# The up products of an MLP by Strassen's algorithm: seven block products in place of eight

## The chip, the cores and the metric

The kernel runs on one core of a Trainium2 chip. A core has a matrix engine (TensorE, PE in the rows), a vector engine (VectorE, DVE), a scalar engine (ScalarE, ACT), a general engine (GpSimd, POOL) and a queue engine (SyncE, SP) that here only starts transfers. Each works off its own instructions strictly in the order in which they stand and waits for the others by semaphores; that order is fixed when the program is built. The metric is the time on the device of one whole execution, in microseconds (us), as the median of several runs.

## The reference, cut to what matters

One decoder block: a gated linear-attention branch and a sparse-attention branch on 512 tokens and 16 extra leading tokens, merged, projected, and then an MLP. The change touches the MLP, and what leads to it:

```python
mix = jnp.einsum('btd,de->bte', merged, w_out[l])
h = h + _rmsnorm(mix, post_mix_norm[l])
n2 = _rmsnorm(h, pre_mlp_norm[l])
u = jnp.square(jax.nn.relu(jnp.einsum('btd,df->btf', n2, w_up[l])))   # 1024 -> 4096
h = h + _rmsnorm(jnp.einsum('btf,fd->btd', u, w_down[l]), post_mlp_norm[l])   # 4096 -> 1024
```

All data are float32. TensorE takes operands of a reduced float32 type, so the kernel splits every operand into a high part (the rounded value) and a low part (what is left) and makes each product of three: high times high, high times low, low times high.

## The kernel before, in words

Everything ahead of the output projection (the attention branches and the merge) is untouched.

**Weights.** `wload` (L90) is how every weight block of 128 x 1024 numbers comes in: SP starts its transfer into one of two `raw` buffers, ScalarE writes the high part (`S.copy`, L99), VectorE writes the low part, `raw` minus high (L100). The pairs lie in five rotating buffers `hl`, or, with `spare`, in two other places.

**Output projection.** `proj_rows` (L517) computes it in two halves of 512 columns. The second half, the tiles `ob`, goes token tile by token tile (four tiles t of 128 tokens); behind each, `mix_done` (L1042) computes the token's norm by a chain of tiny instructions on VectorE and adds the residual into `h2`, and `mix_more` (L1051) transposes the tile on TensorE (`n2t`) and writes it, times the norm weight, as high and low parts `n2h` and `n2l`, in pieces of 128 x 128. The row norm of `n2` itself is applied at the very end (`mlp_scale`, L1065, four more chains of tiny instructions).

**Up.** 4096 hidden columns in four groups g of 1024, each group eight tiles of 128 (`up_tile`, L1094). A tile is 8 x 3 = 24 matmuls with 512 tokens as moving columns: weights of `w_up` stand, `n2` moves. Then ScalarE takes the ReLU out of PSUM (L1106), VectorE squares it (L1108), and `split` makes high and low parts (ScalarE L705, VectorE L706). The first four tiles of group 0 are done in two halves of 256 tokens, so that TensorE can start on the first two token tiles.

**Down.** `down` (L1124) multiplies a group's hidden tiles with `w_down`, 512 output columns at a time, over four accumulators in PSUM (`d`), 24 matmuls of 512 columns each per accumulator, and adds each accumulator into `acc` on VectorE (L1133; group 0 is copied by ScalarE, L1131). The program computes up(0), up(1), down(0), up(2), down(1), up(3), down(2), down(3), so that up is always a group ahead. The last group's second half, the tiles `d3b`, goes token tile by token tile, each with its norm and its output.

**What sets the order.** The calls are recorded in program order; a scheduler then orders the instructions of each engine by that priority, as operands and buffers come free in its own model. Tiles of one tag share that tag's buffers, and a new tile of the tag waits for the last reader of the old one. The tags that matter here: `s1` to `s6` (one large buffer each), `tb` and `st` (two buffers of 128 x 1024 each), `raw` (two), `hl` (five).

Of the kernel before, what the change touches and what calls it, by code (L numbers as in the profile page):

```python
# [38 lines left out]
def hybrid_block(ctx: ExitStack, tc: tile.TileContext, io: dict):  # L39
# [50 lines left out]
    def wload(src, n, name, spare=False):  # L90
# [929 lines left out]
    n2h = mp.tile([P, KT, L], F32R, name="n2h")  # L1020
    n2l = mp.tile([P, KT, L], F32R, name="n2l")
# [28 lines left out]

    def mix_more(t):  # L1051
        nonlocal last_n2

        ts = slice(t * P, (t + 1) * P)
        for b in range(2):
# [4 lines left out]
            for k in range(4):  # L1060
                kk = 4 * b + k
                last_n2 = S.activation(n2h[:, kk, ts], ps[:, k * P : (k + 1) * P], AF.Copy, scale=gmT[:, kk : kk + 1])
                V.scalar_tensor_tensor(n2l[:, kk, ts], ps[:, k * P : (k + 1) * P], gmT[:, kk : kk + 1], f(n2h[:, kk, ts]), ALU.mult, ALU.subtract)

    def mlp_scale(t):  # L1065
        s1 = wk.tile([P, 1], F32, tag="s1", name=f"s1{t}", bufs=2)
        S.activation(gx[:, 2 + t % 2, :], h2[:, t, :], AF.Square, accum_out=s1)
# [26 lines left out]
    def up_tile(g, i, w, c0, n):  # L1094
        uh, ul = us[g]
        nm = f"up{g}{i}{c0}"
        hi, lo = w
        pt = ptile(nm)[:, :n]
        ms = slice(c0, c0 + n)
        for k in range(KT):  # L1100
            ws = slice(k * P, (k + 1) * P)
            TE.matmul(pt, hi[:, ws], n2h[:, k, ms], start=(k == 0), stop=False)  # L1102
            TE.matmul(pt, hi[:, ws], n2l[:, k, ms], start=False, stop=False)  # L1103
            TE.matmul(pt, lo[:, ws], n2h[:, k, ms], start=False, stop=(k == KT - 1))  # L1104
        r = wk.tile([P, T], F32, tag="cv", name=f"r{nm}", bufs=2)[:, :n]
        S.activation(r, pt, AF.Relu)  # L1106
        u = wk.tile([P, T], F32, tag="y", name=f"u{nm}", bufs=2)[:, :n]
        V.tensor_tensor(u, r, r, ALU.mult)  # L1108
        split(uh[:, i, ms], ul[:, i, ms], u)

    def up(g):
        uh = slots.tile([P, 8, L], F32R, tag=("s2", "s6")[g % 2], name=f"uh{g}")
        ul = slots.tile([P, 8, L], F32R, tag=("s1", "s5")[g % 2], name=f"ul{g}")
        us[g] = (uh, ul)
        first = 4 if g == 0 else 0
        ws = [wload(io["w_up"][8 * g + i], 1024, f"up{g}{i}", spare=i % 2 == 1) for i in range(first)]
        for c0 in (0, 256):
            for i in range(first):
                up_tile(g, i, ws[i], c0, 256)
        for i in range(first, 8):  # L1120
            up_tile(g, i, wload(io["w_up"][8 * g + i], 1024, f"up{g}{i}"), 0, L)

    def down(g):
        uh, ul = us[g]  # L1124
        last = g == NG - 1

        def d_evac(pt, t, c0, n, i):
            cs = slice(c0, c0 + n)
            a = acc[t][:, cs]
            if g == 0:  # L1130
# [102 lines left out]
```

## Time and profile before

| what | value |
|---|---|
| median of 3 runs | 1063.04 us (1062.64 to 1063.52) |
| the profiled execution | 1063.86 us, of which span 1062.2 us |
| PE busy | 1040.1 us (98%) |
| DVE busy | 682.0 us (64%) |
| ACT busy | 460.9 us (43%) |
| stretch of the MLP (683 us to the end) | 379 us |

The span runs from the first to the last instruction in the profile; what lies around it is 1063.86 - 1062.2 = 1.7 us. Busy shares are means over the span. Matmuls overlap in the profile (a matmul's duration is longer than the distance to the next one's start), so TensorE's pace is read from the distance of starts, and the same holds for VectorE, where one instruction's end lies over the next one's start.

### The profile page before, as it was taken

To read this page: it belongs to the slowest core of one execution; us is meant where nothing else is said; L and a number is where in the kernel's file an instruction comes from. 1 tells how busy PE (TensorE), PEld (TensorE's weight loads), DVE (VectorE), ACT (ScalarE), POOL (GpSimd) and SP (SyncE) were. 2 spreads that over 40 slices of the span, in tenths; PEclk is the share of its full clock that TensorE was granted. 3 is DMA by queue.
4 is the path that set the end of the run, shared out by engine and by line. 5 is a ranking of instruction groups with operands and counts; after the bars stand their busy time and mean duration, and the time that the engine had idled before them with its cause. 6 is when DMAs were issued, how large, how long until landed. Compare 5 with 4: busy or idle time off the path is not lost.

```text
span 1062.2 us, 15893 instructions
## 1 busy us (share of the span) xinstructions
PE 1040.1 (98%) x6249; PEld 900.7 (85%) x6249; DVE 682.0 (64%) x1502; ACT 460.9 (43%) x854; POOL 61.7 (6%) x85
## 2 busy tenths in 40 slices
PE   6999999999999999999999999999999999999996
PEld 6999999999997888898888888898888888888885
DVE  6797899516789999857967464794431343343346
ACT  5555565443268722346755332473432431242131
POOL 4202302100000000000000000000000000000022
PEclk9999999998999999999999999999999999999999
DMA  5433424210123133322111325133233323332332
GB/s 180 134 102 95 124 86 134 63 41 2 41 83 117 46 94 99 100 80 80 60 60 41 99 93 204 60 103 95 84 96 99 96 85 98 99 90 88 99 99 80
DMA packets 28235, 96.44 MB, mean 91 GB/s; under 512 B 3632, under 2 KB 3968, under 8 KB 28160
## 3 DMA queue, kind: packets, MB, share of 16 engines
q1 hardware_dynamic: 25440, 87.51, 26.5%
q0 software_dynamic: 2720, 7.92, 2.9%
q8 instruction: 49, 0.80, 0.3%
q14 instruction: 26, 0.21, 0.1%
HBM read 90.14 MB, written 5.28 MB: 90 GB/s over the span
## 4 chain that ended last, share of the span: by engine, by line
PE 89%; DVE 5%; ACT 2%; DMA 2%; issue 1%; SPq 0%; DVEq 0%; ACTq 0%
PE up L1103 5%; PE up L1104 5%; PE up L1102 5%; PE d L505 4%; PE d L504 4%; PE d L506 4%; PE pa_dense L891 2%; PE pa_dense L890 2%; PE pa_dense L889 2%; PE pa_q L196 1%; PE pa_q L194 1%; PE pa_q L195 1%; PE pa_bg L194 1%; PE pa_bg L196 1%; PE pa_bg L195 1%; PE bd L1012 1%
## 5 line engine op out<-in xcount | busy, mean ns | idle before, releaser
L1103 PE MATMUL up<-n2l,hi_up 128*128 128x512 f32 (+1 forms) x288 | 106.9, 372 | 0.0
L1102 PE MATMUL up<-n2h,hi_up 128*128 128x512 f32 (+1 forms) x288 | 106.6, 371 | 0.0
L1104 PE MATMUL up<-n2h,lo_up 128*128 128x512 f32 (+1 forms) x288 | 106.6, 371 | 0.0
L100 DVE TENSOR_TENSOR lo_up<-raw_up,hi_up 128x1024 fp32r<-128x1024 f32 x32 | 39.2, 1226 | 71.1 <-PE up L1103 52.9
L100 DVE TENSOR_TENSOR lo_d<-raw_d,hi_d 128x1024 fp32r<-128x1024 f32 x24 | 29.4, 1227 | 78.4 <-PE d L505 56.0
L504 PE MATMUL d<-hi_d,uh 128*128 128x512 f32 x192 | 75.9, 396 | 0.0
L506 PE MATMUL d<-hi_d,ul 128*128 128x512 f32 x192 | 75.9, 395 | 0.0
L505 PE MATMUL d<-lo_d,uh 128*128 128x512 f32 x192 | 75.9, 395 | 0.0
L1106 ACT ACTIVATE rup<-up 128x512 f32<-128x512 f32 (+1 forms) x36 | 19.9, 552 | 99.5 <-PE up L1104 99.4
L1103 PEld LDWEIGHTS up<-n2l,hi_up 128*128 128x128 f32 x288 | 54.2, 188 | 10.3
L1102 PEld LDWEIGHTS up<-n2h,hi_up 128*128 128x128 f32 x288 | 54.2, 188 | 10.3
L1104 PEld LDWEIGHTS up<-n2h,lo_up 128*128 128x128 f32 x288 | 54.1, 188 | 10.3
L99 ACT CAST hi_d<-raw_d 128x1024 fp32r<-128x1024 f32 x24 | 25.2, 1050 | 59.6 <-PE d L506 59.6
L99 ACT CAST hi_up<-raw_up 128x1024 fp32r<-128x1024 f32 x32 | 33.4, 1045 | 24.6 <-PE d L506 22.7
L504 PEld LDWEIGHTS d<-hi_d,uh 128*128 128x128 f32 x192 | 36.1, 188 | 8.8
L506 PEld LDWEIGHTS d<-hi_d,ul 128*128 128x128 f32 x192 | 36.1, 188 | 8.7
L505 PEld LDWEIGHTS d<-lo_d,uh 128*128 128x128 f32 x192 | 36.1, 188 | 8.7
L889 PE MATMUL pa_dense<-nhi,hi_dense 128*128 128x512 f32 x96 | 39.3, 409 | 0.0
L890 PE MATMUL pa_dense<-nlo,hi_dense 128*128 128x512 f32 x96 | 38.0, 396 | 0.0
L548 PE MATMUL pb_z<-hi_z,nhi 128*128 128x256 f32 x128 | 38.0, 297 | 0.0
L891 PE MATMUL pa_dense<-nhi,lo_dense 128*128 128x512 f32 x96 | 38.0, 396 | 0.0
L194 PE MATMUL pa_k<-nhi,hi_k 128*128 128x264 f32 x128 | 37.1, 290 | 0.0
(570 smaller groups left out, 3075.6 us busy)
## 6 DMA issues: line engine op xcount, KB each, us to landing
raw_up<-w_up SPq DMA_DIRECT2D x32, 512.0 KB, 3.6
raw_d<-w_down SPq DMA_DIRECT2D x24, 512.0 KB, 3.6
raw_k<-w_k SPq DMA_DIRECT2D x8, 512.0 KB, 4.6
raw_v<-w_v SPq DMA_DIRECT2D x8, 512.0 KB, 4.4
raw_q<-w_q SPq DMA_DIRECT2D x8, 512.0 KB, 3.6
raw_z<-w_z SPq DMA_DIRECT2D x8, 512.0 KB, 3.6
raw_w_ga<-w_ga SPq DMA_DIRECT2D x8, 512.0 KB, 3.6
raw_bg<-w_bg SPq DMA_DIRECT2D x8, 512.0 KB, 3.6
```

What stands on the lines that cost most here:

```text
L99: S.copy(hi[:, :n], raw[:, :n])
L100: V.tensor_tensor(lo[:, :n], raw[:, :n], f(hi[:, :n]), ALU.subtract)
L194: TE.matmul(pt[:m, :n], hi[:, ws], mh[:, k, ms], start=(k == 0), stop=False)
L504: TE.matmul(pt, lh, whi, start=beg, stop=False)
L505: TE.matmul(pt, lh, wlo, start=False, stop=False)
L506: TE.matmul(pt, ll, whi, start=False, stop=end)
L889: TE.matmul(pt, hi[:, ws], nhi[:, k, NM:], start=(k == 0), stop=False)
L890: TE.matmul(pt, hi[:, ws], nlo[:, k, NM:], start=False, stop=False)
L891: mm = TE.matmul(pt, lo[:, ws], nhi[:, k, NM:], start=False, stop=(k == KT - 1))
L1102: TE.matmul(pt, hi[:, ws], n2h[:, k, ms], start=(k == 0), stop=False)
L1103: TE.matmul(pt, hi[:, ws], n2l[:, k, ms], start=False, stop=False)
L1104: TE.matmul(pt, lo[:, ws], n2h[:, k, ms], start=False, stop=(k == KT - 1))
```

## The change: what it does

Only the MLP's up products, and what makes their operands, change; `down` and the weight loading follow.

A group is now 512 hidden columns, and there are eight. A group's product is cut into 2 x 2 blocks: the weights of `w_up` into four blocks A11, A12, A21, A22 (256 hidden columns by 512 inputs), `n2` into B11, B12, B21, B22 (512 inputs by 256 tokens). Strassen's algorithm in Winograd's form takes seven block products, A11 B11, A12 B21, S1 T1, S2 T2, S3 T3, S4 B22 and A22 T4, in place of eight. S1 to S4 are sums and differences of weight blocks and are made for every group on VectorE: S1 = A21 + A22, S2 = S1 - A11, S3 = A11 - A21, S4 = A12 - S2. T1 to T4 are made once from `n2`. A block product is 2 x 4 x 3 = 24 matmuls of 256 columns. Some of them accumulate onto one another in PSUM (X, Y, Z in the code), with copies taken out by ScalarE in between (`E1`, `E5`, `U`); the four blocks of the result are finished in `hidden`.

Per group, VectorE now makes four sums of 128 x 1024 and seven low parts for up, and four low parts for down; the results of three of the four hidden blocks take an addition more. The sums of `down` over a group go into `acc` twice as often (a group is half as wide), except that groups 0 and 1 share one `down`.

The operand pairs rotate through `pair`: two or three pairs in `hl`, one whose low part is `lo_side`, and from group 2 on one in `side_pair`, so from group 2 on four pairs. The raw weight blocks of groups 2 to 7 lie in `R`, one place for each of the four blocks. `R` takes the tag `s6`, which holds group 1's hidden values before. S1 to S4 are made in one buffer, `Ssum`, of the tag `tb`, which holds two of the four buffers `F` with the blocks of `n2` before. `up` of groups 0 and 1 first makes A11 B11 and A12 B21 of both, which need only the first two token tiles; the last group's down takes the token tiles in the order 2, 3, 0, 1.

The core of the diff:

```diff
+    bop = {x: mp.tile([P, 2, 4, 256], F32R, name=f"bop{x}") for x in ("B11", "B21", "B22", "T1")}
...
+    F = [cst.tile([P, 1024], F32, tag="st", name=f"F0{x}", bufs=2) for x in range(2)] + [wk.tile([P, 1024], F32, tag="tb", name=f"F1{x}", bufs=2) for x in range(2)]
...
+    def operand(x, t, src):
...
+        o = (bop[x] if x in bop else late[x])[:, :, :, t % 2 * P : t % 2 * P + P]
+        S.copy(o[:, 0], src)
+        last_n2 = V.tensor_tensor(o[:, 1], src, f(o[:, 0]), ALU.subtract)
...
     def mix_more(t):
...
-            for k in range(4):
-                kk = 4 * b + k
-                last_n2 = S.activation(n2h[:, kk, ts], ps[:, k * P : (k + 1) * P], AF.Copy, scale=gmT[:, kk : kk + 1])
-                V.scalar_tensor_tensor(n2l[:, kk, ts], ps[:, k * P : (k + 1) * P], gmT[:, kk : kk + 1], f(n2h[:, kk, ts]), ALU.mult, ALU.subtract)
...
+            V.tensor_tensor(fblock(b, t), ps.rearrange("p (k t) -> p k t", t=P), gm, ALU.mult)
+            if t < 2 or b:
+                operand(f"B{b + 1}{t // 2 + 1}", t, fblock(b, t))
+        if t > 1:
+            b11, b21, b12, b22 = (fblock(b, u) for u in (t - 2, t) for b in range(2))
+            V.tensor_tensor(b11, b12, b11, ALU.subtract)
+            operand("T1", t, b11)
+            V.tensor_tensor(b12, b22, b12, ALU.subtract)
+            V.tensor_tensor(b22, b22, b11, ALU.subtract)
+            V.tensor_tensor(b21, b21, b22, ALU.subtract)
...
+    def late_operands():
+        t23 = slots.tile([P, 2, 2, 4, 256], F32R, tag="s1", name="t23")
...
+    def product(pt, w, b, start):
...
+        for m in range(2):
+            o = pt[:, 256 * m : 256 * m + 256]
+            for k in range(4):
+                ws = slice(512 * m + k * P, 512 * m + k * P + P)
+                for i, (x, y) in enumerate(((0, 0), (0, 1), (1, 0))):
+                    TE.matmul(o, w[x][:, ws], b[y][:, k, :], start=start and m + k + i == 0, stop=m == 1 and k == 3 and i == 2, skip_group_check=True)
...
+    def hidden(g, i, j, a, b=None):
...
+            V.tensor_tensor(u, a, b, ALU.add)
+            V.scalar_tensor_tensor(u, u, 0.0, u, ALU.max, ALU.mult)
+        o = us[g][:, :, 2 * i : 2 * i + 2, 256 * j : 256 * j + 256]
+        split(o[:, 0], o[:, 1], u.rearrange("p (a t) -> p a t", t=256))
...
+    def up(g):
...
+            side["S"] = wk.tile([P, 1024], F32, tag="tb", name="Ssum", bufs=2)
...
+        s_ = side["S"]
+        for x in ("11", "21", "22", "12") if not first else ("21", "22", "11", "12"):
+            load(R[x], int(x[0]) - 1, int(x[1]) - 1, g)
+        if not first:
+            X = ptile(f"{nm}X")
+            product(X, parts(R["11"], pair(f"{nm}A11")), bop["B11"], True)
+            E1 = copied(X, "cb", f"E1{g}")
+            us[g] = slots.tile([P, 2, 4, L], F32R, tag="s2", name=f"u{g}")
+        V.tensor_tensor(s_, R["21"], R["22"], ALU.add)
+        Y = ptile(f"{nm}Y")
+        product(Y, parts(s_, pair(f"{nm}S1")), bop["T1"], True)
+        E5 = copied(Y, "ca", f"E5{g}")
+        V.tensor_tensor(s_, s_, R["11"], ALU.subtract)
+        product(X, parts(s_, pair(f"{nm}S2")), late["T2"], False)
+        U = copied(X, "cv", f"U{g}")
+        V.tensor_tensor(s_, R["12"], s_, ALU.subtract)
+        product(Y, parts(s_, pair(f"{nm}S4")), bop["B22"], False)
+        hidden(g, 0, 1, U, Y)
+        V.tensor_tensor(R["21"], R["11"], R["21"], ALU.subtract)
+        product(X, parts(R["21"], pair(f"{nm}S3")), late["T3"], False)
+        hidden(g, 1, 1, E5, X)
+        if not first:
+            Z = ptile(f"{nm}Z")
+            product(Z, parts(R["12"], pair(f"{nm}A12")), bop["B21"], True)
+            hidden(g, 0, 0, E1, Z)
+        product(X, parts(R["22"], pair(f"{nm}A22")), late["T4"], False)
+        hidden(g, 1, 0, X)
...
+    ups = [up(g) for g in range(2)]
+    for _ in range(3):
+        for u in ups:
+            next(u)
+    late_operands()
+    with tc.issue_after(last_n2.ins):
+        for t in range(NT):
+            mlp_scale(t)
+    for u in ups:
+        for _ in u:
+            pass
+    down((0, 1))
+    side["pair"] = quarters_of(slots.tile([P, 4, 1024], F32R, tag="s5", name="side_pair"))[0:2]
...
+    side["R"] = slots.tile([P, 4, 1024], F32, tag="s6", name="R")
+    for g in range(2, NG):
+        for _ in up(g):
+            pass
+        if g < NG - 1:
+            down((g,))
+        else:
+            down_last(g)
```

What it moves is seen in the order of the instructions. The first place is VectorE just ahead of the first product with S1, of group 0 (`Ssum` is S1, L1213 makes it, the last row is its low part; L1061 and L1093 write low parts of T3 and T4, L1223 is S3, the 128x1 rows are norms):

```order
L1061 TENSOR_TENSOR t23_7293<-F01_6729,t23_7293 128x4x128
L1033 TENSOR_SCALAR rv_n20_7310<-s10_7308 128x1
L1033 TENSOR_SCALAR rv_n21_7328<-s11_7326 128x1
L1093 TENSOR_TENSOR t41_7303<-F10_6730,t40_7302 128x4x128 x2
L105 TENSOR_SCALAR t_n20_7313<-rv_n20_7310 128x1
L107 TENSOR_SCALAR h_n20_7314<-rv_n20_7310 128x1
L1213 TENSOR_TENSOR Ssum_7382<-gx_6715 128x1024
L106 TENSOR_SCALAR y_n20_7312<-t_n20_7313 128x1
L1033 TENSOR_SCALAR rv_n22_7346<-s12_7344 128x1
L1223 TENSOR_TENSOR gx_6715<-raw_up011_7380,gx_6715 128x1024
L110 SCALAR_TENSOR_TENSOR t_n20_7313<-y_n20_7312,h_n20_7314 128x1
L701 TENSOR_TENSOR lo_up0S1_7391<-Ssum_7382,hi_up0S1_7390 128x1024
```

The weights of S1 now stand behind all operands of `n2`; before, the weights of the first tiles stood among the pieces of `n2l`, ahead of the last of them.

The second place is VectorE in the up stage of a group in the middle, from the block (0,1) of group 5 to the block (0,0), which the first matmul of the group's down product reads. First the kernel before, at the end of up(1):

```order
L1108 TENSOR_TENSOR uup_7862<-rup_7860 128x512
L706 TENSOR_TENSOR ul_7680<-uup_7862,uh_7679 128x512
L100 TENSOR_TENSOR lo_up_7943<-raw_up_7940,hi_up_7942 128x1024
L1108 TENSOR_TENSOR uup_7899<-rup_7897 128x512
L706 TENSOR_TENSOR ul_7680<-uup_7899,uh_7679 128x512
L100 TENSOR_TENSOR lo_d_7984<-raw_d_7981,hi_d_7983 128x1024
```

Now the changed kernel (`u501`, `u511`, `u500` are the blocks (0,1), (1,1), (0,0) of group 5; L1170 adds, L1171 squares, L701 writes the low part, L98 is the low part of a weight of down):

```order
L1170 TENSOR_TENSOR u501_9185<-U5_9154,up5Y_9097 128x512
L1171 SCALAR_TENSOR_TENSOR u501_9185<-u501_9185 128x512
L98 TENSOR_TENSOR lo_d_9293<-raw_d500_9294,hi_d_9292 128x1024
L701 TENSOR_TENSOR u5_9095<-u501_9185,u5_9095 128x2x256
L1170 TENSOR_TENSOR u511_9219<-E55_9125,up5X_9064 128x512
L1213 TENSOR_TENSOR Ssum_7382<-R_7973 128x1024
L1171 SCALAR_TENSOR_TENSOR u511_9219<-u511_9219 128x512
L98 TENSOR_TENSOR lo_d_9323<-raw_d501_9324,hi_d_9322 128x1024
L701 TENSOR_TENSOR u5_9095<-u511_9219,u5_9095 128x2x256
L1170 TENSOR_TENSOR u500_9252<-E15_9093,up5Z_9224 128x512
L98 TENSOR_TENSOR lo_side_7383<-raw_d510_9361,hi_d_9360 128x1024
L1171 SCALAR_TENSOR_TENSOR u500_9252<-u500_9252 128x512
```

Before, three instructions stand per tile of 24 matmuls of 512 columns; now four and five stand per product of 24 matmuls of 256 columns, among them the next group's S1 and three weights of down.

The third place is SP's queue after groups 0 and 1: the loads of group 2's raw blocks into `R`, behind two loads for down.

```order
L93 DMA raw_d_8208<-w_down 128x1024 [waits DMAHW7_49,DVE_49]
L93 DMA raw_d_8238<-w_down 128x1024 [waits DMAHW0_49,DVE_49]
L1143 DMA R<-w_up 128x2x512 [waits PE_49]
L1143 DMA R<-w_up 128x2x512 x3
L1143 DMA R<-w_up 128x2x512 [waits DMAHW3_49,DVE_49,Activation_49]
```

The first of them waits for TensorE (the last reader of `s6` is down of groups 0 and 1); before, the loads of `w_up` waited for VectorE and ScalarE to be done with a `raw` buffer.

## Rows read from the trace of the kernel before

**Rows 1.** The page, part 1: busy time, share of the span, instructions.

```profile
PE 1040.1 (98%) x6249; PEld 900.7 (85%) x6249; DVE 682.0 (64%) x1502; ACT 460.9 (43%) x854; POOL 61.7 (6%) x85
```

**Rows 2.** Windows: stretch, length, busy of each engine (count), clock, DMA share, GB/s.

```profile
683.00:706.40 23.40, 22.75 (x163) 21.05 (x162) 21.56 (x69) 14.44 (x40) 0.00 (x0) 1.00 0.31 91
727.00:784.00 57.00, 57.00 (x245) 45.83 (x244) 25.21 (x30) 21.59 (x30) 0.00 (x0) 1.00 0.31 93
```

**Rows 3.** Timeline of PE: start, duration, instruction; 69 starts between the two.

```profile
708.55 0.28 PE L1102 MATMUL up<-n2h,hi_up 128*128 128x256 f32 x1
...
716.69 0.39 PE L1102 MATMUL up<-n2h,hi_up 128*128 128x512 f32 x1
```

**Rows 4.** Timeline of ACT: ReLUs of up tiles, three tiles apart.

```profile
767.55 0.60 ACT L1106 ACTIVATE rup<-up 128x512 f32<-128x512 f32 x1 [3.44 <-PE up L1104]
...
784.42 0.60 ACT L1106 ACTIVATE rup<-up 128x512 f32<-128x512 f32 x1 [3.43 <-PE up L1104]
```

**Rows 5.** Groups by shape, from 640 us: busy us, mean ns, idle before.

```profile
L100 DVE TENSOR_TENSOR lo_up<-raw_up,hi_up 128x1024 fp32r<-128x1024 f32 x32 | 39.2, 1226 | 71.1 <-PE up L1103 52.9 <-PE d L505 13.7 <-issue 3.8
L99 ACT CAST hi_up<-raw_up 128x1024 fp32r<-128x1024 f32 x32 | 33.4, 1045 | 24.6 <-PE d L506 22.7 <-DMA raw_up<-w_up 1.8
L706 DVE TENSOR_TENSOR ul<-uup,uh 128x512 fp32r<-128x512 f32 x28 | 19.4, 693 | 19.4 <-ACT uh L705 19.4
L705 ACT CAST uh<-uup 128x512 fp32r<-128x512 f32 x28 | 17.4, 622 | 1.2
L1049 DVE SCALAR_TENSOR_TENSOR h<-h,r,xs 128x512 f32<-128x512 f32 x8 | 5.6, 748 | 0.1
L1133 DVE TENSOR_TENSOR macca<-macca,d 128x512 f32<-128x512 f32 x8 | 5.5, 689 | 4.2 <-PE d L506 4.2
```

**Rows 6.** Timeline of DVE where it never waits: distance of starts.

```profile
690.34 1.22 DVE L100 TENSOR_TENSOR lo_up<-raw_up,hi_up 128x1024 fp32r<-128x1024 f32 x1
691.47 0.15 DVE L1046 TENSOR_SCALAR r<-r 128x1 f32<-128x1 f32 x1
691.53 0.35 DVE L1063 SCALAR_TENSOR_TENSOR n2l<-n2t,gmT,n2h 128x128 fp32r<-128x128 f32 x1
...
1031.09 0.69 DVE L1133 TENSOR_TENSOR maccb<-maccb,d3a 128x512 f32<-128x512 f32 x1 [0.71 <-PE d3a L506]
1031.70 1.22 DVE L100 TENSOR_TENSOR lo_d3b<-raw_d3b,hi_d3b 128x1024 fp32r<-128x1024 f32 x1
```

**Rows 7.** Timelines of PE and DVE at the end of the second `ob` tile.

```profile
678.25 1.03 PE L1059 MATMUL n2t<-ident,h 128*128 128x128 f32 x8
679.04 0.48 PE L504 MATMUL ob<-hi_ob,mhi 128*128 128x512 f32 x1
...
678.44 0.69 DVE L1074 TENSOR_TENSOR h<-ob,gx 128x512 f32<-128x512 f32 x1 [0.39 <-PE ob L506]
```

**Rows 8.** DMA issues by line: KB each, median us to landing.

```profile
raw_up<-w_up SPq DMA_DIRECT2D x32, 512.0 KB, 3.6
...
xs<-x SPq DMA_DIRECT2D x1, 2048.0 KB, 9.3
```

**Rows 9.** Timelines of DVE and PE at the end of the last group.

```profile
1042.31 0.68 DVE L1133 TENSOR_TENSOR macca<-macca,d3b 128x512 f32<-128x512 f32 x1
1047.89 0.69 DVE L1133 TENSOR_TENSOR maccb<-maccb,d3b 128x512 f32<-128x512 f32 x1
1054.13 0.41 DVE L1133 TENSOR_TENSOR maccb<-maccb,d3b 128x256 f32<-128x256 f32 x1
...
1053.26 0.28 PE L506 MATMUL d3b<-hi_d3b,ul 128*128 128x256 f32 x1
```

**Rows 10.** Windows after the last matmul, and PE's timeline at the lower clock.

```profile
1056.00:1062.00 6.00, 0.00 (x0) 0.00 (x0) 2.77 (x10) 0.00 (x0) 0.00 (x0) 0.69 0.24 87
...
240.90 0.41 PE L550 MATMUL pb_z<-hi_z,nlo 128*128 128x256 f32 x1
241.11 0.41 PE L548 MATMUL pb_z<-hi_z,nhi 128*128 128x256 f32 x1
```

More of the change, by code (lines that the diff above doesn't have):

```diff
@@ L1090, in hybrid_block @@
     ss3 = const("ss3", [P, NT, 4])
-    NG = DFF // 1024
+    NG = DFF // 512
     us = {}
[L1094 to L1109, printed above, removed]
@@ L1111, in up @@
-    def up(g):
[L1112 to L1130, printed above, removed]
+    side = {}
+    turn = 0
+    def pair(name):
+        nonlocal turn
+        turn += 1
+        x = turn % (4 if "pair" in side else 3)
+        if x == 3:
+            return side["pair"]
+        hi = wp.tile([P, 1024], F32R, tag="hl", name=f"hi_{name}", bufs=5)
+        return [hi, side["lo"] if x == 2 else wp.tile([P, 1024], F32R, tag="hl", name=f"lo_{name}", bufs=5)]
@@ L1131, in d_evac, with lhs, get, down @@
+    def lhs(gs):
+        def get(k, t):
+            return tuple(us[gs[k // 4]][:, x, k % 4, t * P : (t + 1) * P] for x in range(2))
+        return get
+    def down(gs):
+        g = gs[-1]
+        def evac(pt, t, hf):
+            a = acc[t][:, 512 * hf : 512 * hf + 512]
+            if gs[0] == 0:
                 S.copy(a, pt)
@@ L1149, in out @@
                 nc.sync.dma_start(io["out"][t * P : (t + 1) * P, x], o)
-        def lhs(k, t):
-            return uh[:, k, t * P : (t + 1) * P], ul[:, k, t * P : (t + 1) * P]
-        if last:
-            proj_rows(io["w_down"][g], f"d{g}", lhs, d_evac, out, tail=1)
-        else:
-            for hf in range(2):
-                proj_half(io["w_down"][g][hf], f"d{g}{hf}", lhs, lambda pt, t: d_evac(pt, t, 512 * hf, 512, 0))
-    up(0)
-    for g in range(NG):
-        if g + 1 < NG:
-            up(g + 1)
-        down(g)
+        ws = [[(c, wload(io["w_down"][g // 2][hf][2 * (g % 2) + c], 1024, f"d{g}{hf}{c}", pair("d"))) for c in range(2)] for hf in range(2)]
+        order = (2, 3, 0, 1)
+        for t in order:
+            end = t == order[-1]
+            cuts = (0, 512, 768, 1024) if end else (0, 512, 1024)
+            for i in range(len(cuts) - 1):
+                n, hf = cuts[i + 1] - cuts[i], cuts[i] // 512
+                pt = stile(f"d{g}{t}{i}")[:, :n]
+                rows_part(pt, ws[hf], lhs((g,)), t, slice(cuts[i] - 512 * hf, cuts[i + 1] - 512 * hf))
+                d_evac(pt, t, cuts[i], n, i, end and i == 2)
+            out(t, len(cuts) - 1)
+    ups = [up(g) for g in range(2)]
[11 more added lines that the diff above has]
+    side["pair"] = quarters_of(slots.tile([P, 4, 1024], F32R, tag="s5", name="side_pair"))[0:2]
+    turn = 3
+    side["R"] = slots.tile([P, 4, 1024], F32, tag="s6", name="R")
[4 more added lines that the diff above has]
+            down((g,))
+        else:
+            down_last(g)
     mctx.close()
```

130 lines of the change are left out of this document (94 added, 36 removed).

## The prediction, made before the changed kernel had run

> **What bounds the kernel now.** I read the busy times first, then the windows of the MLP, then the distances of starts on TensorE and VectorE. TensorE is busy for 98% of the span [rows 1]. In a steady stretch of the MLP it never pauses (57.0 of 57.0 us), while VectorE works 25 of 57 us [rows 2]. So fewer matmul columns shorten this kernel as long as nothing else falls behind. But in the stretch where `n2` is made, VectorE works 21.56 of 23.40 us [rows 2], and the change adds to exactly that stretch. The question is whether VectorE can feed seven products as fast as TensorE takes them.
>
> **What it removes.** 69 starts of 256-column matmuls cover 716.69 - 708.55 = 8.14 us, 0.118 us each [rows 3]. Three tiles of 24 matmuls of 512 columns take 784.42 - 767.55 = 16.87 us, 0.2343 us each, 5.62 us per tile [rows 4]. Half the columns cost half the time. Up before is 28 tiles of 5.62 us and 192 half-size matmuls of 0.118 us, 157.5 + 22.7 = 180.1 us; now 8 groups x 7 x 24 = 1344 matmuls of 0.118 us, 158.6 us. TensorE is relieved of 21.5 us; one product takes 2.83 us, seven 19.8 us, and a group's down (96 x 0.2343) stays at 22.5 us.
>
> The page "TensorE: Matmul & The Clock Gate" of the Trainium skill (Back-to-back issue gap) speaks against the change: it says that in a stream of weight loads and matmuls both set the spacing, about 81 ns at 128 columns and 131 ns at 512. On its straight line a 256-column matmul would cost about 98/131 of a 512-column one (an estimate from that page), and up would grow by some 56 us. The rows decide here: 0.118 against 0.2343.
>
> **What a VectorE instruction costs.** Durations are 1.23 us for 1024 wide, 0.69 for 512 wide from SBUF or PSUM, 0.75 for the three-operand form [rows 5]. Neighbours overlap: a 1024-wide one is followed after 1.13 us and a tiny one after 0.06 [rows 6], a 512-wide one after 0.61 [rows 6]. For the three-operand 512 form I take 0.67 (0.75 less the same overlap). The new forms (a product with a broadcast out of PSUM, a maximum times itself, strided halves) do not occur before; the nearest rows are 0.69 and 0.75, and I take these; below that lies nothing in the rows, above it 4 pieces of 0.35 us for the same 512 columns [rows 6].
>
> **Term 1, the first product with S1.** It needs T1 of all tokens and S1, and S1's buffer is free only after the operands of T4 have been read from it. In VectorE's order, 37 additions of 512, 7 of 1024, 8 three-operand instructions of 512 and 43 tiny ones stand from the evacuation of the second `ob` tile (start 678.44 [rows 7]) to S1's low part of group 0. That is 22.6 + 7.9 + 5.4 + 43 x 0.12 (between 0.06 and about 0.19) = 41 us, so 719.5; with about 1.5 us of waits for casts and transposes, 721. In the same time TensorE, from 678.25 [rows 7], has two `ob` tiles (11.2), four transposed tiles (4 x 0.79 = 3.2) and four products (11.3): 704. It stands still for 17 us, partly ahead of the transposes, which wait for the same VectorE. Before, it stood for 0.65 us there (23.40 - 22.75 [rows 2]). Cost 16.3 us.
>
> **Term 2, the rest of groups 0 and 1.** Ten products, 28.3 us. VectorE has, from S1 to the last weight of group 1, 15 instructions of 1024, 6 of 512, 2 three-operand and 41 tiny ones: 17.0 + 3.7 + 1.3 + 4.9 = 26.9 us, and it must do them by turns with TensorE. Walking through, I find three waits: S1 of group 1 stands behind two hidden blocks of group 0 (4 us), then its S2 (1.2) and S4 (0.7); with the start of the first product about 7 us. I keep 3 to 12.
>
> **Term 3, R.** The four loads into `R` wait for the last matmul of down of groups 0 and 1. A block lands 3.6 us after its issue, and four blocks' bytes take 9.3 us [rows 8], so one more every 1.9 us: 3.6, 5.5, 7.4, 9.3. A cast (1.05 [rows 5]) lets the first matmul go at 4.7. S1 is made at 7.4 + 1.13; then sum, cast and low part follow on each other: S1's pair at 10.9, S2's at 14.3, S4's at 18.9. The last 96 matmuls (11.3 us) flow from about 18: the up stage ends at 29.4 instead of 19.8. Cost 9.6 us; 5 if the later sums hide, 13 if blocks in 2-KB pieces load slower than these rows.
>
> **Term 4, the turn from up to down.** In groups 2 to 6 the first matmul of down reads block (0,0). From the end of the S4 product VectorE must issue the 12 instructions that the order shows: 5 of 512, 4 of 1024, 3 three-operand, 3.1 + 4.5 + 2.0 = 9.6 us, and with 0.2 us to start, 0.15 where one waits for its neighbour, and ScalarE's cast (0.62 [rows 5]) 10.6 us. TensorE arrives after three products, 8.5 us. It waits 2.1 us, in groups 3 to 6 8.5 us. In group 2, where A12 comes earlier, but VectorE is late, I find 2.3 and 1.3 more at its low part. Together 12 us (0 to 20). Group 7 begins with token tiles 2 and 3, whose blocks are ready: nothing.
>
> **Term 5, the end.** Before, a token tile takes VectorE 1047.89 - 1042.31 = 5.58 us [rows 9], as long as its 24 matmuls (5.62). Now each tile has one addition more (0.61), 6.2 us, and falls behind by 0.6 at each of three: the last addition starts 2.2 us behind the last matmul instead of 0.8 (1054.13 against 1053.26 and a pitch of 0.12 [rows 9]). Cost 1.4 us.
>
> **Term 6, TensorE's clock.** After the last matmul the granted clock falls to half within the tail (0.69 over 6 us [rows 10]); at 1.2 GHz a 256-column matmul takes 0.21 us [rows 10] in place of 0.118. The unbroken part of Term 1's pause, behind the last of the four products, is about 11 us, longer than the whole tail of 1062.2 - 1053.4 = 8.8 us, so S1's product should begin at the low level; each product there costs 2.2 us more. Most of that lies beside VectorE's queue, which is late anyway. I take 2 us (0 to 8). The same page of the Trainium skill (Loop structure matters more than you think) says that a long wait between bursts of matmuls lets the clock fall; by it Term 3 pays too.
>
> ScalarE makes more casts too, but has hardly half of VectorE's load and hides; loads for the output projection stand behind two more blocks in SP's queue, about 2 us later, which the projection's first half covers, else up to 2 us.
>
> **Sum.** 1062.2 - 21.5 + 16.3 + 7 + 9.6 + 12 + 1.4 + 2 = 1089.0 us of span. The median of runs stands 1063.04 - 1062.2 = 0.8 us above the span, so 1089.8; I say 1089.
>
> **Rivals.**
> *TensorE stays fed* (faster). The unbroken stream of matmuls [rows 2] speaks for it: 1062.2 - 21.5 + 1.4 + 0.8 = 1043. It decides if the 95 instructions of Term 1 take VectorE under 27 us instead of 41 and the loads of `R` go out earlier; the dense stretch of before, 92% busy, and the wait for TensorE in SP's order speak against it. With Term 3 alone it is 1053. Chance 0.09.
> *Only the structural waits* (about no change up to somewhat slower). Terms 1 and 3 are paid, but by half, and the turns hide: 1043 + 8 + 5 to 1043 + 16 + 10, 1056 to 1069, in the middle 1063. For it: VectorE idles more than half of the steady stretch [rows 2]. Against it: at the turn it is an ordered queue that counts, not the mean. Chance 0.13, a third of it within 0.2% of before and a tenth of it faster.
> *The waits chain* (slower still). Each pause brings the half clock, products at 5.1 us delay VectorE's hidden blocks, which delay the next sums: Terms 2, 3, 4 and 6 at their upper ends, 5 + 3.4 + 8 + 6 more, 1112. Chance 0.13.
>
> **How the numbers follow.** The forecast has 0.65, with a range of its own of 1076 to 1101. What a measurement of this kernel can tell from no change is about 0.2%, 2.1 us. Faster takes the first rival and a tenth of the second: 0.10. Same, a third of the second and the edge of its rest: 0.05. Slower is what is left, 0.85. The range 1062 to 1107 leaves out the first rival and the far end of the last, under 0.2 together.
>
> **What would show it.** In the profile after: 2 x 24 matmul starts of a product 0.118 us apart; a hole in TensorE of over 8 us ahead of the first product on `bopT1`, with VectorE full; a hole of 4 to 6 us behind down of groups 0 and 1, ended by a DMA into `R`; a hole of about 2 us ahead of the first down matmul in groups 2 to 6, ended by ScalarE's cast of `u`, and none in group 7. Wrong it would be if these holes are filled, or if a group from 3 to 6 takes under 43 us in place of 44.4.

## The result, and the profile after

The changed kernel takes 1095.07 us (median of 4 runs, 1091.46 to 1096.09) against 1063.28 for the kernel before on the same chip: ratio 1.0288, 95% interval 1.0258 to 1.0317. The forecast was 1089 with a range of 1062 to 1107 and 0.85 on slower. The profiled execution has a span of 1093.5 us, 31.3 more than before.

The head of the page after, which answers to [rows 1]:

```profile
span 1093.5 us, 16951 instructions
PE 1034.0 (95%) x6717; PEld 919.9 (84%) x6717; DVE 784.4 (72%) x1596; ACT 482.4 (44%) x852; POOL 62.2 (6%) x85
```

TensorE's share fell from 98% to 95%: it now stands still. Its busy time fell by only 6.1 us, in part because products at the low clock are long. Where it stands still, by what ended the wait, from 660 us on (total us, times, longest):

```profile
PE d L502 <- ACT u L700: 10.6, 5, 3.3
PE up0Y L1156 <- ACT hi_up0S L700: 9.1, 1, 9.1
PE up2X L1156 <- ACT hi_up2A L700: 5.1, 1, 5.1
PE up1Y L1156 <- DVE lo_up1S L701: 2.6, 1, 2.6
PE up1Z L1156 <- DVE hl L701: 2.1, 1, 2.1
```

The first row is the five turns from up to down, the second the first product with S1, the third group 2's first block out of `R`, the last two lie in groups 0 and 1. Windows of the same trace (columns as in [rows 2]); the first is the dense stretch, the next two single products, the last the start of group 5's down:

```profile
683.00:725.00 42.00, 28.44 (x183) 25.51 (x182) 41.25 (x99) 20.18 (x34) 0.00 (x0) 0.88 0.21 63
...
718.50:724.50 6.00, 5.34 (x26) 5.05 (x27) 5.89 (x18) 1.04 (x1) 0.00 (x0) 0.57 0.28 87
...
806.60:812.70 6.10, 5.64 (x25) 5.34 (x26) 5.30 (x5) 1.04 (x1) 0.00 (x0) 0.52 0.37 139
...
969.50:973.50 4.00, 4.00 (x11) 3.20 (x12) 3.41 (x4) 1.55 (x2) 0.00 (x0) 0.58 0.38 119
```

VectorE works 41.25 of 42.0 us in the first, as forecast. The second and third are the first products behind the two long pauses: granted clock 0.57 and 0.52, and 5.8 and 6.0 us for a product that takes 2.82 elsewhere. 0.5 is the level of 1.2 GHz and 1.00 that of 2.4; a value between them is a mean over a window that has both. TensorE's timeline shows that pace, the hole ahead of `R`, and one turn (start, duration, engine, line, operation; in brackets the idle time before it):

```profile
801.04 0.40 PE L504 MATMUL d<-hi_d,u 128*128 128x512 f32 x1
806.55 0.80 PE L1156 MATMUL up2X<-bopB,hi_up2A 128*128 128x256 f32 x2 [5.11 <-ACT hi_up2A L700]
...
861.87 0.40 PE L1156 MATMUL up3Y<-bopT,hi_up3S 128*128 128x256 f32 x2
...
864.69 0.40 PE L1156 MATMUL up3X<-t,hi_up3S 128*128 128x256 f32 x2
...
880.86 0.50 PE L502 MATMUL d<-hi_d,u 128*128 128x512 f32 x1 [1.81 <-ACT u L700]
```

From 861.87 to 864.69 is one product, 2.82 us as counted from [rows 3]. The wait ahead of `R` is put down to ScalarE's cast, but that cast itself waited for the transfer; the other two rows are VectorE's last step of S2 of group 0 and of S1 of group 2, which "Why the prediction was right" uses:

```profile
805.45 1.04 ACT L700 CAST hi_up2A<-R 128x1024 fp32r<-128x1024 f32 x1 [3.39 <-DMA R<-w_up]
...
722.39 1.21 DVE L701 TENSOR_TENSOR lo_side<-Ssum,hi_up0S 128x1024 fp32r<-128x1024 f32 x1
...
810.88 1.22 DVE L701 TENSOR_TENSOR lo_up2S<-Ssum,hi_up2S 128x1024 fp32r<-128x1024 f32 x1
```

At the end, VectorE's additions of the last down (L1257) and pairs of final three-operand instructions (L1271), then GpSimd's multiplications by the norm weight beside them:

```profile
1070.37 0.67 DVE L1257 TENSOR_TENSOR maccb<-maccb,d 128x512 f32<-128x512 f32 x1
...
1075.12 2.47 DVE L1271 SCALAR_TENSOR_TENSOR maccb<-maccb,r,h 128x512 f32<-128x512 f32 x2
1077.51 0.68 DVE L1257 TENSOR_TENSOR macca<-macca,d 128x512 f32<-128x512 f32 x1
...
1071.94 1.30 POOL L1263 TENSOR_TENSOR maccb<-maccb,gfin 128x512 f32<-128x512 f32 x1 [2.04 <-ACT jd L1262]
1075.20 1.84 POOL L1263 TENSOR_TENSOR macca<-macca,gfin 128x512 f32<-128x512 f32 x1 [1.96 <-ACT jd L1262]
```

And the same in the kernel before, one multiplication per token tile:

```profile
1044.66 0.54 DVE L112 SCALAR_TENSOR_TENSOR t_fin<-y_fin,h_fin 128x1 f32<-128x1 f32 x1
1046.53 1.41 DVE L1148 SCALAR_TENSOR_TENSOR macca<-macca,r,h 128x512 f32<-128x512 f32 x2
...
1043.89 1.30 POOL L1140 TENSOR_TENSOR macca<-macca,gfin 128x512 f32<-128x512 f32 x1 [4.32 <-ACT jd L1139]
```

A token tile takes VectorE 7.1 us (1077.51 - 1070.37), against 5.58 before [rows 9]; the pair takes 2.47 instead of 1.41. TensorE's last matmul ends at 1080.1, 13.4 us before the end, against 8.7 before (1062.2 - 1053.54 [rows 9]).

### The profile page after: what moved, and what is told of

Read it like the earlier page. It is cut to its first block, busy times and chain, and to the rows that moved or that the text cites. A ratio compares the mean times of both kernels' runs of the same rounds, so it can differ in the third digit from the quotient of the medians.

```text
span 1093.5 us, 16951 instructions
## 1 busy us (share of the span) xinstructions
PE 1034.0 (95%) x6717; PEld 919.9 (84%) x6717; DVE 784.4 (72%) x1596; ACT 482.4 (44%) x852; POOL 62.2 (6%) x85
## 4 chain that ended last, share of the span: by engine, by line
PE 78%; DVE 13%; DMA 3%; ACT 3%; issue 2%; SPq 0%; DVEq 0%; ACTq 0%
PE d L502 5%; PE d L503 5%; PE d L504 5%; PE pa_dense L886 2%; PE pa_dense L885 2%; PE pa_dense L884 2%; PE pb_z L543 1%; PE pa_q L192 1%; PE pa_q L194 1%; PE pa_bg L192 1%; PE pa_q L193 1%; PE pa_bg L193 1%; PE bd L1006 1%; PE bd L1007 1%; PE bd L1005 1%
## 5 line engine op out<-in xcount | busy, mean ns | idle before, releaser
L502 PE MATMUL d<-hi_d,u 128*128 128x512 f32 (+1 forms) x212 | 84.1, 397 | 5.5 <-ACT u L700 5.5
L504 PE MATMUL d<-hi_d,u 128*128 128x512 f32 (+1 forms) x212 | 82.9, 393 | 0.0
L503 PE MATMUL d<-lo_d,u 128*128 128x512 f32 (+1 forms) x140 | 54.9, 392 | 0.0
L502 PEld LDWEIGHTS d<-hi_d,u 128*128 128x128 f32 x212 | 40.3, 190 | 15.1 <-ACT u L700 6.1
L504 PEld LDWEIGHTS d<-hi_d,u 128*128 128x128 f32 x212 | 40.1, 189 | 9.4
L884 PE MATMUL pa_dense<-nhi,hi_dense 128*128 128x512 f32 x96 | 39.3, 409 | 0.0
L97 ACT CAST hi_d<-raw_d 128x1024 fp32r<-128x1024 f32 x26 | 27.3, 1050 | 25.3 <-PE d L503 12.7
L192 PE MATMUL pa_v<-nhi,hi_v 128*128 128x264 f32 x128 | 37.0, 289 | 0.0
L192 PE MATMUL pa_q<-nhi,hi_q 128*128 128x258 f32 x128 | 36.8, 287 | 0.0
L194 PE MATMUL pa_k<-nhi,lo_k 128*128 128x264 f32 x128 | 36.7, 288 | 0.0
L544 PE MATMUL pb_z<-lo_z,nhi 128*128 128x256 f32 x128 | 36.6, 286 | 0.0
L545 PE MATMUL pb_z<-hi_z,nlo 128*128 128x256 f32 x128 | 36.4, 285 | 0.0
L194 PE MATMUL pa_v<-nhi,lo_v 128*128 128x264 f32 x128 | 36.4, 284 | 0.0
L193 PE MATMUL pa_v<-nlo,hi_v 128*128 128x264 f32 x128 | 36.4, 284 | 0.0
```

What stands on the lines that cost most here:

```text
L192: TE.matmul(pt[:m, :n], hi[:, ws], mh[:, k, ms], start=(k == 0), stop=False)
L193: TE.matmul(pt[:m, :n], hi[:, ws], ml[:, k, ms], start=False, stop=False)
L194: mark = TE.matmul(pt[:m, :n], lo[:, ws], mh[:, k, ms], start=False, stop=(k == KT - 1))
L502: TE.matmul(pt, lh, whi, start=beg, stop=False)
L503: TE.matmul(pt, lh, wlo, start=False, stop=False)
L504: TE.matmul(pt, ll, whi, start=False, stop=end)
```

## The experiments

Each time below is the median of 4 or 5 runs (12 in the last experiment). The kernel before ran beside them, with a median of 1063.3 to 1063.7 us; each ratio is to it, with its 95% interval in brackets. Differences to the changed kernel go by its 1095.07, which has a spread of its own (1091.46 to 1096.09). Comments in the code are added here.

**The turn.** `down` of groups 2 to 6 takes the token tiles in another order:

```diff
-            for t in range(NT):
+            for t in order:              # (2, 3, 0, 1) for a single group
                 rows_part(pts[t], [(c, w)], lhs, t, ...)
```

> The down products of groups 2 to 6 take the token tiles in the order 2, 3, 0, 1; nothing else changes. Theory (an ordered queue, Term 4): the five holes ahead of down, 3.26 + 1.81 + 1.81 + 1.86 + 1.88 = 10.6 us, are there because the first matmul asks for block (0,0); tiles 2 and 3 ask for blocks that were ready two products earlier, and block (0,0) then has 2.8 us more. The holes go, and with them the fall of the clock behind one of them (1.5 us): about 1083 to 1085 in place of 1095, periods of groups 3 to 6 of 42.4 us. Rival (VectorE late by a fixed amount): the hole appears again ahead of the next group's first sum, time within 3 us of 1095.

Measured: 1080.31 us, ratio 1.0156 (1.0141 to 1.0171), 14.8 less than the changed kernel. The row `d L502 <- ACT u` is gone and the others stand; the first three waits of this kernel:

```profile
PE up0Y L1156 <- ACT hi_up0S L700: 9.2, 1, 9.2
PE up2X L1156 <- ACT hi_up2A L700: 5.1, 1, 5.1
PE up1Y L1156 <- DVE lo_up1S L701: 2.8, 1, 2.8
```

Nothing came back elsewhere. The gain is more than the holes: down of group 2 takes 22.6 us instead of 25.3 and that of group 5 no longer 24.1, since the low clock behind their holes is gone too: 10.6 + 2.8 + 1.5 = 14.9. The expected 1083 to 1085 had counted the slower clock behind one hole alone.

**R.** Group 2 uses the buffers that group 1 used:

```diff
-            R = {x: side["R"][:, i, :] for i, x in enumerate(...)}
+            R = {x: side["R"][:, i, :] ...} if g > 2 else {"21": gx[:, 2, :], "22": gx[:, 3, :]}
+            for x in () if g > 2 else ("11", "12"):
+                R[x] = wp.tile([P, 1024], F32, tag="raw", ...)
...
+        if g == 3:  # side_pair and R begin here
```

> Group 2 takes its blocks from the two quarters and the two raw buffers that group 1 used, so none of its loads waits for the last matmul of down of groups 0 and 1; R begins with group 3. Theory (Term 3, a buffer): the hole of 5.11 us behind that down goes, the first product and the down that began at the low clock (6.2 and 25.3 us) take 2.8 and 22.5, and S1 to S4 no longer follow loads: 8 to 12 us less, 1083 to 1087. Rival (loads and VectorE are late in any case): the hole turns up one product later, time within 3 us of 1095.

Measured: 1080.64 us, 1.0165 (1.0151 to 1.0179), 14.4 less. Two waits of this kernel, and its window of 800 to 840 us:

```profile
PE up0Y L1156 <- ACT hi_up0S L700: 9.1, 1, 9.1
PE d L502 <- ACT u L700: 7.3, 4, 1.9
```

```profile
800.00:840.00 40.00, 39.69 (x253) 35.36 (x252) 25.45 (x29) 16.53 (x22) 0.00 (x0) 1.00 0.42 132
```

The hole is gone, group 2's seven products take 20.0 us (802.45 to 822.42) instead of 29.1, and its turn, the longest of the five, went with it (4 in place of 5): VectorE was late there because the loads were. That is 9.1 + 3.3 + 2.1 (its down at the full clock), above the 8 to 12 expected, which had left out the turn.

**The start.** S1 of group 0 ahead of the late operands, in a free buffer; and, apart from it, `mlp_scale` behind the products of groups 0 and 1:

```diff
-        s_ = side["S"]
+        s_ = gpost if first else side["S"]
...
+    next(ups[0])                        # S1's product of group 0
     late_operands()
```

```diff
-    with tc.issue_after(last_n2.ins):
-        for t in range(NT):
-            mlp_scale(t)
     for u in ups: ...
+    for t in range(NT):
+        mlp_scale(t)
     down((0, 1))
```

> S1 of group 0 is made in a free quarter of another buffer, and its product stands ahead of the operands of T2, T3 and T4. Theory (Terms 1 and 2, VectorE is full there, so the length of its queue counts): the product of S1 moves into TensorE's pause, and what is gained is only what TensorE no longer does behind VectorE's queue: 2 to 5 us, 1090 to 1093. Rival (the wait for the buffer alone is the cost): the pause of 9.1 us goes nearly whole, 1085 to 1087. Third: VectorE decides and nothing moves, 1095.

> The changed kernel, with the four norm chains of mlp_scale recorded behind the products of groups 0 and 1; in VectorE's order the two tiny instructions ahead of S1 and the 12 between S1's sum and the low part of S2 then stand behind. Theory (Term 1 counts every instruction in VectorE's queue, a tiny one 0.06 to 0.19 us): S1's product begins about 1 us earlier and S2's about 2 us, 1093 to 1094. Rival (the chains wait for each other's results and cost far more than their pitch): the start moves by 4 us or more, under 1092.

Measured: 1093.51 (1.0280, 1.0260 to 1.0301) and 1093.52 (1.0283, 1.0269 to 1.0297); neither differs from the changed kernel by more than its interval. In the first, S1's product lies in the pause, as intended, and the pause simply stands behind it, ahead of S2:

```profile
PE up0X L1156 <- ACT hi_up0S L700: 6.8, 1, 6.8
```

From the first product to the last of group 1 it is 66.5 us (690.49 to 756.98), as in the changed kernel (691.32 to 757.80; 67.8 and 68.3 in the two runs above). The second takes 65.0. So neither one buffer nor the order of one block made that stretch long; moving work within VectorE's queue gains 0 to 3 us. The rivals, that the buffer's wait (1085 to 1087) or the norm chains (under 1092) are the cost, fell; whether 1 to 5 us were gained or nothing can't be told apart at this precision.

**The end.** First, ScalarE multiplies by the norm and GpSimd adds the residual for tokens 2, 3 and 0 (below); then the same with VectorE adding (`V` in place of `G`); then GpSimd's multiplication by the norm weight left out.

```diff
-                V.scalar_tensor_tensor(o, o, r3, h2[:, t, x], ALU.mult, ALU.add)
+                if n == 2:
+                    S.activation(o, o, AF.Copy, scale=r3)
+                    G.tensor_tensor(o, o, h2[:, t, x], ALU.add)
+                else:
+                    V.scalar_tensor_tensor(o, o, r3, h2[:, t, x], ALU.mult, ALU.add)
```

```diff
-            G.tensor_tensor(a, a, gfin[c0 // 512][...], ALU.mult)
```

> In the last down, ScalarE multiplies tokens 2, 3 and 0 by their norm and GpSimd adds the residual; only the last token tile keeps VectorE's form. Theory (Term 5: VectorE's 7.1 us per token tile against 5.6 us of matmuls): VectorE has about 4.7 us per tile, does not fall behind, and the tail from the last matmul to the end falls from 13.4 to about 9: 3 to 4.7 us less, 1090 to 1092. Rival (GpSimd and VectorE slow each other in any instruction): what is taken from VectorE comes back as longer additions, within 1.5 us of 1095.

> As the run before on the last down, but the residual of tokens 2, 3 and 0 is added by VectorE's plain two-operand addition; GpSimd keeps only the multiplications by the norm weight. Theory (VectorE's three-operand form waits until a running GpSimd instruction ends; its two-operand additions do not): per token tile VectorE has two additions into acc, 13 tiny ones and two additions of 512 without waits, 5.2 to 6.0 us instead of 6.8; the tail is 9 to 11 us, 1090 to 1091. Rival (GpSimd slows every VectorE instruction): the period stays at 6.8 or more, 1091 to 1094.

> Leaves out the multiplications by the norm weight on GpSimd in the last down (the output lacks that factor); all else is the changed kernel. Theory (GpSimd's instructions stretch VectorE's three-operand ones): the pair of final three-operand instructions takes 1.4 us instead of 2.46, the period per token tile falls from 7.1 to 6.1 or 6.2, as the prediction counted it, and the tail from 13.4 to about 10.2: 3 us less, 1092. Rival (the added addition alone makes VectorE late): the period stays near 7, time within 1 us of 1095.

Measured: 1091.34 (1.0270, 1.0254 to 1.0285), 1093.17 (1.0286, 1.0271 to 1.0301) and 1090.11 (1.0251, 1.0237 to 1.0265). By the traces the tail from the last matmul is 12.5, 13.0 and 8.95 us. The first two theories fell: there the period stayed at 6.8, and what the first saves in time lies mostly ahead of the tail: the first addition of its last group starts 3.0 us earlier than in the changed kernel (1060.29 against 1063.29), before the edit acts, since the downs of groups 2 and 5 ran less at the low clock in that execution (24.1 and 22.6 us against 25.3 and 24.1, behind about the same holes). VectorE in the first of them, and GpSimd beside it:

```profile
1074.41 0.15 DVE L106 TENSOR_SCALAR y_fin<-t_fin 128x1 int32<-128x1 int32 x1
1074.60 1.09 DVE L110 SCALAR_TENSOR_TENSOR t_fin<-y_fin,h_fin 128x1 f32<-128x1 f32 x1
1075.72 1.20 DVE L114 SCALAR_TENSOR_TENSOR y_fin<-t_fin,y_fin 128x1 f32<-128x1 f32 x1
1076.96 0.22 DVE L110 SCALAR_TENSOR_TENSOR t_fin<-y_fin,h_fin 128x1 f32<-128x1 f32 x1
1077.10 0.68 DVE L1257 TENSOR_TENSOR macca<-macca,d 128x512 f32<-128x512 f32 x1
```

```profile
1073.13 2.54 POOL L1273 TENSOR_TENSOR maccb<-maccb,h 128x512 f32<-128x512 f32 x2
1075.63 1.28 POOL L1263 TENSOR_TENSOR macca<-macca,gfin 128x512 f32<-128x512 f32 x1
```

A three-operand instruction of one column lasts until GpSimd's instruction ends (1075.69 and 1075.67; 1076.92 and 1076.91), and takes 0.22 when none runs; the one-operand one ahead takes 0.15 while GpSimd works. The Trainium skill, "SBUF — State Buffer" (SBUF: two separate sides), says that a VectorE instruction with two SBUF inputs and a GpSimd one that reads SBUF share a port pair, and that whichever starts first keeps it for its whole length; the trace agrees. It also shows why the second form fell: its two-operand additions of the residual have both inputs in SBUF, and the first of a pair waits for GpSimd too (1070.73 is where GpSimd ends; such a pair takes 1.30 without it). The additions into `acc`, whose other input is in PSUM, stay at 0.68.

```profile
1070.10 1.78 DVE L1273 TENSOR_TENSOR maccb<-maccb,h 128x512 f32<-128x512 f32 x2 [0.85 <-ACT maccb L1272]
...
1069.43 1.30 POOL L1263 TENSOR_TENSOR maccb<-maccb,gfin 128x512 f32<-128x512 f32 x1 [1.96 <-ACT jd L1262]
```

Without GpSimd's work the period is 5.69 and the pair 1.41 (the kernel that leaves the multiplication out):

```profile
1071.04 1.41 DVE L1270 SCALAR_TENSOR_TENSOR maccb<-maccb,r,h 128x512 f32<-128x512 f32 x2
1072.37 0.68 DVE L1257 TENSOR_TENSOR macca<-macca,d 128x512 f32<-128x512 f32 x1
...
1076.73 1.41 DVE L1270 SCALAR_TENSOR_TENSOR macca<-macca,r,h 128x512 f32<-128x512 f32 x2
1078.06 0.75 DVE L1257 TENSOR_TENSOR macca<-macca,d 128x256 f32<-128x256 f32 x2
```

That is better than the 6.1 to 6.2 and 1092 expected. So the tail's growth is mostly the second GpSimd multiplication per token tile, which now starts together with VectorE's final pair (1075.20 and 1075.12) and makes it 1.05 us longer. The addition that the change adds costs less than its 0.61: 5.58, less the 0.32 that one tiny instruction waits for GpSimd in the kernel before (0.54 in place of 0.22), and 5.69 without any such wait leave about 0.4 us for it.

**All four together** (turn, R, S1, the second form of the end).

> Token order of down, buffers of group 2, S1 of group 0 ahead, and ScalarE's scaling in the last down, all together. Theory (each hole has its own cause): what is left of the prediction's terms is the start, about 16 to 20 us of Terms 1 and 2 with the half clock there, so 1043 + 18 + 3, 1062 to 1070, about as before. Sum of the single savings, with group 2's turn and its low clock counted once: 14.8 + 14.5 - 5.4 + 1.6 + 4, 29.5 less, 1065. Rival (waits only shift, VectorE's total is too long): over 1075.

Measured: 1069.97 us, 1.0062 (1.0049 to 1.0075): at the upper end of what the theory said, and 5 us above the sum of the single savings. The holes have separate causes; what is left is the start (65.9 us where 14 products are 39.5) and the tail.

**Eight products for groups 0 and 1.** Nothing then needs sums ahead of the first products, and T1 to T4 are made while they run. B12 needs a place (quarters of `s5`), `R` follows there, `u` of groups 0 and 1 trade places. The turn is as above, `mlp_scale` stands behind group 1, and the end is the second form. In the second kernel the late operands are held back behind the last B operand; in the third the last two groups' down is one again, so that the first 512 columns are added and multiplied before the end, and VectorE's final pair is the changed kernel's again.

```diff
+        for n, (i, j) in enumerate(((0, 0), (1, 0), (1, 1), (0, 1)) if g == 0 else ((0, 0), (0, 1), (1, 0), (1, 1))):
+            X = ptile(f"up{g}{i}{j}", pp if n < 2 else sp)
+            for k in range(2):
+                w = block(i, k)
+                b = f"B{k + 1}{j + 1}"
+                product(X, w, bop[b] if b in bop else late[b], k == 0, k == 1)
+            hidden(g, i, j, X)
...
+    up_plain(0)
+    with tc.issue_after(last_n2.ins):   # second and third kernel
+        late_operands()
+    up_plain(1)
...
+        elif g < 7:                     # third kernel
+            down((5,), (g - 5,))        # one half behind up(5), one behind up(6)
+        else:
+            down_last((6, 7))
```

> Groups 0 and 1 take the eight block products, with no sums of operands ahead of them, and the sums are made while these run; groups 2 to 7 keep seven products; R lies where group 1 has long been done; token order of down and the last down as in the runs before. Theory (Terms 1 and 2 are VectorE's queue for the operands T and S, where TensorE has nothing else to do): two more products, 5.7 us, buy 18 to 23 us: 1062.2 - 21.5 + 5.7 + 2 to 5 of the tail and the start + 0.8, 1047 to 1053, faster than before by 0.9 to 1.4%. Rival (the stretch is too dense for VectorE in any form): TensorE stands still for 8 us or more ahead of tokens 2 and 3, 1057 or more.

> As the run with eight products in groups 0 and 1, but every operand T is held back until the last operand B of tokens 3 has been issued. Theory (VectorE's queue again: six instructions of 512, 3.7 us, stood ahead of the operands of token tile 3): the holes of 2.29 and 0.66 us there go, and with them the product at the low clock (5.57 in place of 2.8): 4 to 5.5 us less, 1053.5 to 1055. Rival (the norm chain of token tile 3 and its transposes set the time): 0 to 1 us, 1058.

> As the run before, and the last two groups' down is one again: down of group 5 is cut in two halves around up of group 6, down of groups 6 and 7 takes its first 512 columns for all tokens ahead, so a token tile at the end has one addition on VectorE, as in the kernel before the change. Theory (Term 5 is VectorE's work per token tile against its matmuls): the tail from the last matmul falls from 12.9 to about 8.8, 4 us less than the run before, 1049 to 1051. Rival (GpSimd's overlap alone makes the tail long): 12 us or more, about the run before.

Measured: 1058.96 (0.9960, 0.9946 to 0.9973), 1054.07 (0.9911, 0.9897 to 0.9924) and 1050.53 us (0.9878, 0.9864 to 0.9891): 1.2% faster than the kernel before. The first missed its 1047 to 1053: its waits show why, and the second's that the hold cured it.

```profile
PE up L1159 <- ACT bx L1065: 2.3, 1, 2.3
PE d L504 <- DVE u L701: 0.9, 2, 0.5
PE n2t L1074 <- DVE h L1046: 0.7, 1, 0.7
```

```profile
PE n2t L1074 <- DVE h L1046: 0.4, 1, 0.4
PE d L504 <- DVE u L701: 0.4, 1, 0.4
```

A wait of 2.3 us had cost 4.9: the product behind it took 5.4 us (granted clock 0.70 from 708.3 to 714 us). The third kernel's dense stretch, and VectorE in its last down:

```profile
683.00:706.00 23.00, 22.67 (x162) 20.80 (x161) 22.05 (x51) 12.44 (x19) 0.54 (x1) 1.00 0.39 125
706.00:725.00 19.00, 19.00 (x162) 19.00 (x161) 18.66 (x44) 13.40 (x24) 0.00 (x0) 1.00 0.19 58
```

```profile
1026.85 1.41 DVE L1271 SCALAR_TENSOR_TENSOR macca<-macca,r,h 128x512 f32<-128x512 f32 x2
1028.18 0.68 DVE L1257 TENSOR_TENSOR macca<-macca,d 128x512 f32<-128x512 f32 x1
...
1033.71 0.68 DVE L1257 TENSOR_TENSOR maccb<-maccb,d 128x512 f32<-128x512 f32 x1
```

TensorE is fed where VectorE still works 40.7 of 42 us; the clock stays at 1.00. From the first product to the first matmul of down it is 48.2 us (690.25 to 738.46), where 16 products and 16 transposes are 46.7. So a full VectorE alone doesn't hold TensorE up; it did where TensorE had nothing to do until VectorE came to its next operand. The period at the end is 5.53 and the tail 8.6 us, though GpSimd multiplies here too: once per token tile, beside the tiny instructions and done before the pair.

**What the seven products are worth.** The third kernel with eight products everywhere:

> The run before with eight block products in groups 2 to 7 as well, no sums of blocks (operand T1 stands in for B12, which has no room there, so the output is not the reference's; the work is the same). It tells what the seven products are worth where TensorE is fed. Theory: 6 more products of 2.82 us, 17 us, all on the path: 1066 to 1069. Rival (TensorE has hidden slack, or VectorE's sums cost TensorE what the eighth product would): under 1060.

Measured: 1064.24 us, 1.0008 (0.9998 to 1.0017). Six products cost 13.7 us, less than the 17 and the 1066 to 1069 expected (the rival, under 1060, fell too): in the seven-product form small waits and longer downs (23.1 and 23.9 us in groups 2 and 4) and 19.9 to 20.3 us for the products of groups 3 to 7 in place of 19.8 give some 3 us back. So the other edits are worth nothing beside the kernel before, and the whole gain is the algorithm's, once TensorE is fed.

## Why the prediction was right, and where it was off

By the spans, term by term, predicted and read from the trace after (us):

| step | predicted | measured |
|---|---|---|
| relief | -21.5 | a product 2.82, as counted |
| Terms 1 and 2, groups 0 and 1 | +23.3 | +23.5: 66.5 from first to last product, less 42.4 of products, transposes and five matmuls of down, less 0.65 before |
| Term 3, R | +9.6 | +9.3: 801.44 to 830.58, less 19.8 |
| Term 4, the turns | +12 | +10.6 |
| Term 5, the end | +1.4 | +4.7 |
| Term 6, the clock beside these | +2 | +4.3: down of groups 2 and 5 |
| sum | +26.8 | +30.9 of 31.3 |

Terms 1 and 2: right in size. That VectorE's queue ahead of TensorE's next operand is the cause, and not one wait, is shown by the runs: reordering moved the hole and gained 0 to 3 us, while taking the sums out of that stretch left 1.5 us of the 23.5. Within the two terms the match is partly luck: S1's product began 2.5 us sooner than the 721 forecast, and what followed took 2.8 longer (39.3 us to 757.80, less 28.3 of products and 1.2 of five matmuls of down, 9.8 against 7). The three waits of Term 2 came as 2.6, nothing and 0.2 us in place of 4, 1.2 and 0.7; waits of 1.1 and 0.7 ahead of other products and the half clock fill the rest.

Term 3 and Term 4: right, and shown one by one by two edits that change no amount of work. In Term 3 the walk itself holds: VectorE had finished S1's, S2's and S4's pairs of group 2 at 10.7, 14.3 and 18.9 us after the last matmul of down (forecast 10.9, 14.3 and 18.9). In Term 4 the holes are 1.8 to 1.9 us in groups 3 to 6 (forecast 2.1), and groups 3, 4 and 6 take 44.2 to 44.3 us (forecast 44.4). The two are not additive with the clock nor with each other: group 2's turn came from `R`.

Term 5 failed in its reason: "Now each tile has one addition more (0.61), 6.2 us". The pitch of 5.58 [rows 9] held one GpSimd multiplication beside the norm's tiny instructions; the second one of a token tile falls on VectorE's final pair: 7.1, and 5.69 without GpSimd.

Term 6 was mis-sized for this execution. The two pauses over 5 us and the one of 2.6 were followed by a product at the low level, and that share lies in the other terms, beside VectorE's queue, as the prediction said: the slow products ended at 724.3 and 812.6, and the next ones' low parts were only done at 723.6 and 812.1 (rows above). What the prediction did not count is the downs behind the turns, 4.3 us here; in the three runs that change only the last down they lost 1.6, 4.3 and 1.6 us.

The rival *only the structural waits* (1063) fell because the turns did not hide and Terms 1 and 3 came in full; *the waits chain* (1112) because the holes have separate causes, each cured alone, and the half clock behind the long pauses mostly lay beside VectorE's queue. *TensorE stays fed* (1043) could be had, but only with other schedules: 1050.5, with 5.7 us of extra products.

## What to carry to other kernels

Trading matmuls for additions paid here only where TensorE was fed: look at the densest stretch of VectorE, and try the plain form there. A hole costs itself and often slow matmuls behind it, so small reorderings (which block a consumer reads first, which buffer a load waits for) gave 14 us each here, some 5 of them the same ones. Read which other engine ran during a duration before carrying it into a sum.

## What was not expected of the hardware

A hole of 1.85 us in group 5 was followed by about 3.3 us of half clock (0.58 in the window of 969.5 to 973.5 us), while three holes of 1.8 to 1.9 us in groups 3, 4 and 6 were not. Neither the hole's length nor its place in the kernel decides it: in the runs that change only the last down, the same hole of group 5 left the clock at 1.00 (from 968 to 972 us with GpSimd adding the residual), and with VectorE adding it, the fall came behind group 6's hole of 1.88 us instead:

```profile
968.00:972.00 4.00, 4.00 (x17) 3.26 (x18) 3.36 (x4) 1.43 (x2) 0.00 (x0) 1.00 0.31 116
...
1015.00:1019.00 4.00, 4.00 (x11) 3.21 (x12) 3.36 (x4) 1.50 (x2) 0.00 (x0) 0.57 0.34 119
```

What tells them apart stays open; it is part of why executions of one kernel differ by some microseconds here. And a VectorE instruction of a single column took 1.2 us beside GpSimd.
